# Attention with a bias: a dozen products moved from VectorE to GpSimd, a reordered start and a reordered end

## The chip, the cores and the metric

The kernel runs on one core of a Trainium2 chip. The metric is the device time of one execution in microseconds, lower is better. Times below are medians of several runs. Runs of one kernel agree within 1%, most far closer, with an exception that matters below: the kernel before took about 256.3 us instead of 253.6 in 7 of 31 runs.

The engines are called as the profile calls them: PE is TensorE (PEld its weight loads), ACT is ScalarE, DVE is VectorE, POOL is GpSimd, SP is SyncE.

## The reference

Batch 4, 8 heads, sequence 1024, head size 64. All heads share one bias.

```python
scores = scale * np.matmul(q, k.transpose(0, 1, 3, 2))
scores = scores + bias
scores_max = np.max(scores, axis=-1, keepdims=True)
attn = np.exp(scores - scores_max) / (np.sum(np.exp(scores - scores_max), axis=-1, keepdims=True) + 1e-8)
return np.matmul(attn, v)
```

The kernel uses exp(s + b) = exp(s) * exp(b). It computes exp(bias) once, stores it in `eb`, and multiplies every block of exponentials by it. The row sum comes from a column of ones beside V.

## The kernel before

The unit of work is a bank: 128 keys by 512 queries of one head. There are 512 banks, in groups of 16 (one head pair and one half of the queries; the two heads alternate). ACT exponentiates three banks at a time (a slot), DVE multiplies two at a time (a pair), and PE multiplies each bank with V.

```python
banks = [(pr, h, qh, kc) for pr in range(NP) for qh in range(2) for kc in range(NCH) for h in range(2)]
slots = [[0], [1, 2]] + [list(range(i, min(i + 3, NB))) for i in range(3, NB, 3)]
...
def s_fill(g):                        # PE: scores of one slot into PSUM, two slots deep
    for j, b in enumerate(slots[g]):
        nc.tensor.matmul(ps[:, j, :], kT[:, kc, :], qT[:, h, qh * HQ:(qh + 1) * HQ], start=True, stop=True)

def s_exp(g):                         # ACT: exponential, PSUM to SBUF
    nc.scalar.activation(e_at(slots[g][0], n), open_ps.pop(("S", g))[:, :n, :], ACTF.Exp, scale=scale)

def mul_pair(b, n=2):                 # DVE: two SBUF inputs, 128 x 1024 bf16
    e = e_at(b, n)
    nc.vector.tensor_tensor(e, e, eb[:, qh, kc:kc + 1, :].to_broadcast([P, n, HQ]), op=ALU.mult)
...
for i in range(8):                    # prologue: warm-up matmuls
    nc.tensor.matmul(wm[:, i % 3, :], zeros[:, :P], zeros[:], start=True, stop=True)
...                                   # k_first, q_first: casts, transposes and copies of the first blocks
k_first(0, nc.scalar.copy, nc.scalar.copy)
q_first(0, nc.vector.tensor_copy)
s_fill(0)
s_exp(0)
q_first(1, nc.vector.tensor_copy)
s_fill(1)
s_exp(1)
k_first(2, nc.vector.tensor_copy, nc.vector.tensor_copy)
```

The order of everything after the prologue is found while the program is written: a small model with a clock for ACT, PE and DVE picks the next instruction of each engine. Each engine then runs its list in order, so an instruction that comes late holds up all that stand behind it on its engine.

The softmax here doesn't subtract the row's maximum and nothing guards it: scores larger than these inputs give would overflow.

## Time and profile before

| | before |
|---|---|
| time, median of 3 (range) | 253.62 us (253.60 to 253.69) |
| span of the profiled run (which took 254.24 us) | 252.5 us |
| first exponential begins | 6.20 us |
| three-bank exponentials without a gap from | 8.96 us, three banks done |
| last exponential ends | 244.74 us |
| from there to the end | 7.8 us |

These are two lines of the page's list of groups. The columns after the bar are busy microseconds and the mean ns of one instruction, then the idle time in front of the group and what ended it.

```profile
L130 ACT ACTIVATE E<-ps 128x1536 bf16<-128x1536 f32 (+2 forms) x172 | 230.1, 1668 | 2.1 <-PE ps L125 2.1
L148 DVE TENSOR_TENSOR E<-E,eb 128x1024 bf16<-128x1024 bf16 x256 | 163.5, 683 | 1.0 <-ACT eb L143 1.0
```

ACT's exponentials of scores waited only 2.1 us in the whole run. A product lasts 0.68 us, but overlaps the next: 163.5 / 256 = 0.64 us of busy time each, and a new one can begin every 0.60 us.

The windows view of the kernel before gives busy microseconds and, in brackets, instructions of each engine in a stretch of 30 us.

```profile
core 0: us, PE busy (x) PEld busy (x) DVE busy (x) ACT busy (x) POOL busy (x), PEclk, DMA share, GB/s
60.00:90.00 30.00, 28.38 (x386) 17.19 (x392) 28.69 (x59) 30.00 (x23) 6.33 (x8) 1.00 0.65 91
210.00:240.00 30.00, 28.30 (x388) 17.97 (x391) 29.08 (x60) 30.00 (x24) 0.00 (x0) 1.00 0.13 49
```

ACT is the bound, at 30.00 of 30. DVE with 28.7 to 29.1 has almost no slack.

The start, from the timelines of PE and ACT before (start, duration, engine, line, operation, output and input, count, idle time in front):

```profile
1.23 3.40 PE L209 MATMUL wm<-zeros 128*128 128x512 bf16 x8 [1.23 <-DVE zeros L184]
4.56 0.30 PE L217 MATMUL px<-ident,kr 128*64 128x128 bf16 x4
7.86 1.06 PE L125 MATMUL ps<-qT,kT 128*128 128x512 bf16 x3
```

```profile
6.20 0.60 ACT L130 ACTIVATE E<-ps 128x512 bf16<-128x512 f32 x1 [0.92 <-PE ps L125]
7.65 1.02 ACT L130 ACTIVATE E<-ps 128x1024 bf16<-128x1024 f32 x1 [0.85 <-PE ps L125]
8.96 6.82 ACT L130 ACTIVATE E<-ps 128x1536 bf16<-128x1536 f32 x5 [0.28 <-PE ps L125]
```

And the end, from its timeline:

```profile
243.42 1.32 ACT L130 ACTIVATE E<-ps 128x1024 bf16<-128x1024 f32 x1
244.47 3.09 DVE L148 TENSOR_TENSOR E<-E,eb 128x1024 bf16<-128x1024 bf16 x5
247.62 0.42 PE L160 MATMUL po<-vall,E 128*128 128x65 bf16 x8 [0.19 <-DVE E L148]
```

When ACT is done at 244.74 us, DVE still has almost all of five products before it. They, not the last exponential, set the end.

### The profile page before, as it was taken

How to read it: one execution, taken by the hardware profiler on the slowest of the kernel's cores; microseconds unless marked ns; L12 is line 12 of the kernel's file. 1: busy time of each engine (PE TensorE's matmuls, PEld its weight loads, DVE VectorE, ACT ScalarE, POOL GpSimd, SP SyncE). 2: the span in 40 equal slices, each digit the busy share in tenths (PEclk: the TensorE clock that was granted, in tenths of full speed). 3: DMA queues.
4: the chain of work that ended last, by engine and by line, in shares of the span. 5: the costliest groups of instructions: out<-in, count | busy, mean ns of one | idle time of the engine just before them, and what ended most of it. 6: DMA issues, size and time to landing. Idle time of an engine off the chain costs nothing.

```text
span 252.5 us, 7217 instructions
## 1 busy us (share of the span) xinstructions
PE 229.4 (91%) x3090; PEld 141.6 (56%) x3144; DVE 226.3 (90%) x461; ACT 239.1 (95%) x180; POOL 52.6 (21%) x72
## 2 busy tenths in 40 slices
PE   7768999999999999999999999999999999999982
PEld 2346646665565566565555566565555655555651
DVE  5319799999999999999999999999999999999993
ACT  3899999999999999999999999999999999999970
POOL 6652445022310513013042204034000000000000
PEclk9999999999999999999999999999999999999998
DMA  7999999749291589439196904939020201111112
GB/s 147 171 214 187 191 138 161 90 106 104 66 148 40 105 67 150 64 71 139 42 141 47 187 8 95 118 85 166 5 84 3 86 0 44 44 43 44 49 36 83
DMA packets 47744, 23.79 MB, mean 94 GB/s; under 512 B 34401, under 2 KB 43361, under 8 KB 47457
## 3 DMA queue, kind: packets, MB, share of 16 engines
q0 software_dynamic: 42272, 14.42, 52.7%
q1 hardware_dynamic: 5296, 8.78, 9.6%
q8 instruction: 24, 0.39, 0.7%
q10 hardware_dynamic: 144, 0.13, 0.2%
q14 instruction: 8, 0.06, 0.1%
HBM read 29.36 MB, written 8.39 MB: 150 GB/s over the span
## 4 chain that ended last, share of the span: by engine, by line
PE 44%; ACT 35%; DVE 10%; DMA 4%; issue 3%; POOL 1%; ACTq 1%
ACT E L130 33%; PE ps L125 30%; PE po L160 8%; DVE E L148 6%; PE px L88 6%; DMA qr<-in_q_dram 4%; ACT eb L143 2%; DVE oall L171 1%; DVE qT L97 1%; POOL vall L80 1%; DVE mask L199 1%; DVE rs L170 1%; ACTq L130 1%; PE pb L138 0%; POOL kr L74 0%
## 5 line engine op out<-in xcount | busy, mean ns | idle before, releaser
L130 ACT ACTIVATE E<-ps 128x1536 bf16<-128x1536 f32 (+2 forms) x172 | 230.1, 1668 | 2.1 <-PE ps L125 2.1
L148 DVE TENSOR_TENSOR E<-E,eb 128x1024 bf16<-128x1024 bf16 x256 | 163.5, 683 | 1.0 <-ACT eb L143 1.0
L125 PE MATMUL ps<-qT,kT 128*128 128x512 bf16 x458 | 134.5, 378 | 12.9 <-ACT E L130 4.7
L160 PEld LDWEIGHTS <-E 128*128 128x128 bf16 x2048 | 84.7, 98 | 40.3 <-DVE E L148 2.6
L160 PE MATMUL po<-vall,E 128*128 128x65 bf16 x2048 | 96.4, 194 | 2.4 <-DVE E L148 1.0
L125 PEld LDWEIGHTS <-kT 128*128 128x128 bf16 x512 | 45.3, 96 | 43.1 <-issue 10.2
L74 POOL DMA_DIRECT2D kr<-in_k_dram x15 | 10.5, 699 | 96.4 <-PE px L88 91.5
L171 DVE TENSOR_TENSOR oall<-po,rs 128x256 f32<-128x256 f32 x64 | 27.2, 425 | 2.4 <-DVE rs L170 0.3
L80 POOL DMA_DIRECT2D vall<-in_v_dram x32 | 28.1, 882 | 6.0 <-DMA btraw<-in_bias_dram 4.0
L97 DVE TENSOR_TENSOR qT<-px,mask 128x1024 bf16<-128x1024 bf16 x31 | 21.3, 688 | 2.3 <-PE px L88 1.6
L101 DVE COPY kT<-px 128x512 bf16<-128x512 bf16 x31 | 13.1, 424 | 10.5 <-PE px L88 9.7
L75 POOL DMA_DIRECT2D qr<-in_q_dram x15 | 10.7, 716 | 17.3 <-PE px L88 16.7
L170 DVE RECIPROCAL rs<-po 128x4 f32<-128x4 f32 x64 | 11.4, 179 | 3.1 <-PE po L160 2.7
L88 PE MATMUL px<-ident,qr 128*64 128x128 bf16 x248 | 12.8, 224 | 1.0 <-DMA qr<-in_q_dram 0.9
L88 PE MATMUL px<-ident,kr 128*64 128x128 bf16 x248 | 12.8, 225 | 0.2
L88 PEld LDWEIGHTS <-kr 128*64 128x64 bf16 x248 | 7.9, 109 | 8.5 <-issue 5.2
L88 PEld LDWEIGHTS <-qr 128*64 128x64 bf16 x248 | 8.0, 109 | 8.2 <-issue 6.4
L143 ACT ACTIVATE eb<-pb 128x2048 bf16<-128x2048 bf16 x4 | 7.5, 1881 | 0.6 <-PE pb L138 0.6
L138 PE MATMUL pb<-ident,btraw 128*128 128x128 bf16 x64 | 4.6, 225 | 0.9 <-ACT E L130 0.7
L138 PEld LDWEIGHTS <-btraw 128*128 128x128 bf16 x64 | 4.5, 147 | 1.5 <-issue 1.2
L209 PE MATMUL wm<-zeros 128*128 128x512 bf16 x8 | 3.4, 607 | 1.2 <-DVE zeros L184 1.2
L209 PEld LDWEIGHTS <-zeros 128*128 128x128 bf16 x8 | 1.0, 142 | 2.9 <-issue 1.6
(27 smaller groups left out, 13.3 us busy)
## 6 DMA issues: line engine op xcount, KB each, us to landing
out_dram<-oall SPq DMA_DIRECT2D x32, 256.0 KB, 2.5
vall<-in_v_dram POOLq DMA_DIRECT2D x32, 128.0 KB, 6.0
kr<-in_k_dram POOLq DMA_DIRECT2D x15, 256.0 KB, 4.2
qr<-in_q_dram POOLq DMA_DIRECT2D x15, 256.0 KB, 5.2
btraw<-in_bias_dram POOLq DMA_DIRECT2D x2, 1024.0 KB, 12.6
k0f<-in_k_dram SPq DMA_DIRECT2D x2, 128.0 KB, 3.3
q0f<-in_q_dram ACTq DMA_DIRECT2D x1, 128.0 KB, 2.5
q0f<-in_q_dram SPq DMA_DIRECT2D x1, 128.0 KB, 2.6
```

The costliest lines, as they stand in the source:

```text
L75: nc.gpsimd.dma_start(out=qr.rearrange("p t c d -> p t (c d)"), in_=qf[pr])
L80: nc.gpsimd.dma_start(out=vall[:, 2 * pr + t, :, :D], in_=vf[pr, :, t])
L88: nc.tensor.transpose(px[t * D:(t + 1) * D, c, :], src[:, t, half * QC + c, :], ident[:])
L97: nc.vector.tensor_tensor(dst[:, :, half * HQ:(half + 1) * HQ], px.rearrange("p c q -> p (c q)").unsqueeze(1).to_broadcast([P, 2, HQ]), ma ...
L101: nc.vector.tensor_copy(dst[:, half * QC:(half + 1) * QC, :], px[:])
L125: nc.tensor.matmul(ps[:, j, :], kT[:, kc, :], qT[:, h, qh * HQ:(qh + 1) * HQ], start=True, stop=True)
L130: nc.scalar.activation(e_at(slots[g][0], n), open_ps.pop(("S", g))[:, :n, :], ACTF.Exp, scale=scale)
L143: nc.scalar.activation(eb[:, qh, k0:k0 + 4, :], open_ps.pop(("B", qh, k0))[:, :4, :], ACTF.Exp)
L148: nc.vector.tensor_tensor(e, e, eb[:, qh, kc:kc + 1, :].to_broadcast([P, n, HQ]), op=ALU.mult)
L160: nc.tensor.matmul(acc[:, i, :], e[:, 0, i * P:(i + 1) * P], vall[:, 2 * pr + h, kc, :], start=(kc == 0 and i == 0), stop=(kc == NCH - 1), ...
L170: nc.vector.reciprocal(rs[:], acc[:, :, D:D1])
L171: nc.vector.tensor_tensor(oall[:, qh * QC:(qh + 1) * QC, :], acc[:, :, :D], rs[:].to_broadcast([P, QC, D]), op=ALU.mult)
```

## The change

The intent: begin ACT's stream earlier, take enough products from DVE that it finishes with ACT, and shorten what follows the last exponential. The core of the diff (cuts marked):

```diff
+    banks[NB - 16:] = [(NP - 1, h, 1, kc) for h in range(2) for kc in range(NCH)]
+    late_bias = {NB - 2: 0, NB - 1: 1}
+    slots = [[0], [1, 2], [3]] + [list(range(i, min(i + 3, NB))) for i in range(4, NB, 3)]
...
+            if b in late_bias:
+                nc.tensor.matmul(ps[:, j, :], ident[:], braw[:, late_bias[b], :], start=False, stop=True)
...
-    def mul_pair(b, n=2):
+    def mul_pair(b, n=2, eng=nc.vector):
...
+            if b == NB - 1:                      # last evacuation: half DVE and SP, half ACT
+                m = QC // 2
+                nc.vector.tensor_tensor(oall[:, c0:c0 + m, :], acc[:, :m, :D], ...)
+                nc.sync.dma_start(...)
+                for i in range(m, QC):
+                    nc.scalar.mul(oall[:, c0 + i, :], acc[:, i, :D], rs[:, i, :])
+                nc.scalar.dma_start(...)
...
-        for i in range(8):
+        for i in range(6):
             nc.tensor.matmul(wm[:, i % 3, :], zeros[:, :P], zeros[:], start=True, stop=True)
...
+        k_first(0, nc.scalar.copy, nc.scalar.copy, "xb")
+        c_a = q_first(0, "xa")
+        c_b = q_first(1, "xb")
+        c_a()
+        c_b()
         s_fill(0)
         s_exp(0)
+        k_first(2, nc.vector.tensor_copy, nc.vector.tensor_copy, "xa")
+        for g in range(1, 3):
+            s_fill(g)
+            s_exp(g)
...
+        def pool_pick():                         # DVE three pairs behind: the last of them to GpSimd
+            b, n, last = mul_next, 0, None
+            while b + 1 in exp_at and banks[b][2:] in eb_at:
+                if b not in pool_has and max(exp_at[b + 1], eb_at[banks[b][2:]]) <= max(t_pool, t_dve):
+                    n, last = n + 1, b
+                b += 2
+            if n < 3:
+                return None
+            ...
+                mul_pair(b, eng=nc.gpsimd)
+                mul_at[b] = mul_at[b + 1] = t + POOLMUL      # POOLMUL = 2100 ns
```

The model gives GpSimd a clock of its own.

More of the change, by code (lines that the diff above doesn't have):

```diff
@@ L60 @@
     eb = consts.tile([P, 2, NCH, HQ], BF)
+    braw = consts.tile([P, 2, HQ], BF)
     mask = consts.tile([P, 2, HQ], BF)
@@ L106 @@
     NB = len(banks)
-    slots = [[0], [1, 2]] + [list(range(i, min(i + 3, NB))) for i in range(3, NB, 3)]
+    banks[NB - 16:] = [(NP - 1, h, 1, kc) for h in range(2) for kc in range(NCH)]
+    late_bias = {NB - 2: 0, NB - 1: 1}
+    slots = [[0], [1, 2], [3]] + [list(range(i, min(i + 3, NB))) for i in range(4, NB, 3)]
     NS = len(slots)
@@ L112, in e_at @@
     def e_at(b, n):
+        b = b + 2
         if b // ET not in etiles:
@@ L125, in s_fill @@
             nc.tensor.matmul(ps[:, j, :], kT[:, kc, :], qT[:, h, qh * HQ:(qh + 1) * HQ],
-                             start=True, stop=True)
+                             start=True, stop=b not in late_bias)
+            if b in late_bias:
+                nc.tensor.matmul(ps[:, j, :], ident[:], braw[:, late_bias[b], :], start=False, stop=True)
     def s_exp(g):
@@ L143, in b_exp, with late_bias_pe, copy @@
         nc.scalar.activation(eb[:, qh, k0:k0 + 4, :], open_ps.pop(("B", qh, k0))[:, :4, :], ACTF.Exp)
-    def mul_pair(b, n=2):
+    def mul_pair(b, n=2, eng=nc.vector):
         pr, h, qh, kc = banks[b]
         e = e_at(b, n)
-        nc.vector.tensor_tensor(e, e, eb[:, qh, kc:kc + 1, :].to_broadcast([P, n, HQ]), op=ALU.mult)
+        if banks[b + 1][1] == h:
+            eng.tensor_tensor(e, e, eb[:, qh, kc:kc + n, :], op=ALU.mult)
+        else:
+            eng.tensor_tensor(e, e, eb[:, qh, kc:kc + 1, :].to_broadcast([P, n, HQ]), op=ALU.mult)
+    def late_bias_pe(tag):
+        px = ps_x.tile([P, 2, HQ], BF, tag=tag, name="px")
+        for j in range(2):
+            for i in range(QC):
+                nc.tensor.transpose(px[:, j, i * P:(i + 1) * P],
+                                    btraw[:, QC + i, :].rearrange("p (kp kc) -> p kc kp", kc=NCH)[:, NCH - 2 + j, :],
+                                    ident[:])
+        def copy():
+            nc.vector.tensor_scalar(braw[:], px[:], 1.0 / scale, None, op0=ALU.mult)
+        return copy
     oalls = {}
@@ L170, in evac @@
             nc.vector.reciprocal(rs[:], acc[:, :, D:D1])
-            nc.vector.tensor_tensor(oall[:, qh * QC:(qh + 1) * QC, :], acc[:, :, :D],
+            c0 = qh * QC
+            if b == NB - 1:
+                m = QC // 2
+                nc.vector.tensor_tensor(oall[:, c0:c0 + m, :], acc[:, :m, :D],
+                                        rs[:, :m, :].to_broadcast([P, m, D]), op=ALU.mult)
+                nc.sync.dma_start(out=of[2 * pr + h][:, c0:c0 + m, :], in_=oall[:, c0:c0 + m, :])
+                for i in range(m, QC):
+                    nc.scalar.mul(oall[:, c0 + i, :], acc[:, i, :D], rs[:, i, :])
+                nc.scalar.dma_start(out=of[2 * pr + h][:, c0 + m:c0 + QC, :], in_=oall[:, c0 + m:c0 + QC, :])
+                return
+            nc.vector.tensor_tensor(oall[:, c0:c0 + QC, :], acc[:, :, :D],
                                     rs[:].to_broadcast([P, QC, D]), op=ALU.mult)
-            if qh == 1:
+            if pr == NP - 1:
+                nc.sync.dma_start(out=of[2 * pr + h][:, c0:c0 + QC, :], in_=oall[:, c0:c0 + QC, :])
+            elif qh == 1:
                 nc.sync.dma_start(out=of[2 * pr + h], in_=oall[:])
@@ L207, with k_first @@
         wm = ps_s.tile([P, 3, HQ], F32, tag="s", name="wm")
-        for i in range(8):
+        for i in range(6):
             nc.tensor.matmul(wm[:, i % 3, :], zeros[:, :P], zeros[:], start=True, stop=True)
-        def k_first(c0, cast, copy):
+        def k_first(c0, eng_cast, eng_copy, tag):
             cs = slice(c0, c0 + 2)
-            cast(kr0[:, :, cs, :], k0f[:, :, cs, :])
-            px = ps_x.tile([P, 2, P], BF, tag="xb", name="px")
+            eng_cast(kr0[:, :, cs, :], k0f[:, :, cs, :])
+            px = ps_x.tile([P, 2, P], BF, tag=tag, name="px")
             for c in range(2):
@@ L217, in k_first, with q_first @@
                     nc.tensor.transpose(px[t * D:(t + 1) * D, c, :], kr0[:, t, c0 + c, :], ident[:])
-            copy(kT0[:, cs, :], px[:])
-        def q_first(t, copy):
+            eng_copy(kT0[:, cs, :], px[:])
+        def q_first(t, tag):
             nc.vector.tensor_copy(qr0[:, t, :QC, :], q0f[t][:])
-            px = ps_x.tile([P, QC, P], BF, tag="xa", name="px")
+            px = ps_x.tile([P, QC, P], BF, tag=tag, name="px")
             for c in range(QC):
                 nc.tensor.transpose(px[t * D:(t + 1) * D, c, :], qr0[:, t, c, :], ident[:])
-            copy(qT0[t * D:(t + 1) * D, t, :HQ], px[t * D:(t + 1) * D, :, :].rearrange("p c q -> p (c q)"))
-        k_first(0, nc.scalar.copy, nc.scalar.copy)
-        q_first(0, nc.vector.tensor_copy)
+            return lambda: nc.vector.tensor_copy(qT0[t * D:(t + 1) * D, t, :HQ],
+                                                 px[t * D:(t + 1) * D, :, :].rearrange("p c q -> p (c q)"))
+        k_first(0, nc.scalar.copy, nc.scalar.copy, "xb")
[3 more added lines that the diff above has]
+        c_b()
         s_fill(0)
         s_exp(0)
-        q_first(1, nc.vector.tensor_copy)
-        s_fill(1)
-        s_exp(1)
-        k_first(2, nc.vector.tensor_copy, nc.vector.tensor_copy)
+        k_first(2, nc.vector.tensor_copy, nc.vector.tensor_copy, "xa")
+        for g in range(1, 3):
+            s_fill(g)
+            s_exp(g)
         EXP, EXP0, QK, AV, TP = 427, 45, 216, 170, 350
         MUL, COPYQ, COPYK, EVAC, SEM = 600, 650, 420, 620, 80
-        order = [("S", g) for g in range(2, NS)]
+        POOLMUL = 2100
+        order = [("S", g) for g in range(3, NS)]
         for at, x in ((5, (0, 0)), (7, (0, 4)), (11, (1, 0)), (13, (1, 4))):
@@ L243 @@
         NO = len(order)
-        T0 = 9000.0
-        t_act, t_pe, t_dve = T0 + 900, T0, T0
+        T0 = 7500.0
+        t_act, t_pe, t_dve = T0 + 700, T0, T0 + 500
         filled = []
         act_end = []
-        x_free = {"xa": T0, "xb": T0}
+        x_free = {"xa": T0 + 500, "xb": T0}
         x_unit = {}
         bias_at = [13500, 22000]
-        raw_at = {0: 7000, 1: 17500, 2: 27500}
+        raw_at = {0: (6000, 7500), 1: (17200, 18300), 2: (26000, 28500)}
         pieces = [(0, 1, 1), (0, 0, 1)]
@@ L254 @@
             pieces += [(pr, 1, 0), (pr, 0, 0), (pr, 1, 1), (pr, 0, 1)]
+        pieces.append((NP, 0, 0))
+        raw_at[NP] = (T0, T0)
         piece_end = {(0, 1, 0): T0, (0, 0, 0): T0}
         eb_at = {}
-        exp_at = {0: T0 + 400, 1: T0 + 900, 2: T0 + 900}
+        exp_at = {0: T0, 1: T0 + 700, 2: T0 + 700, 3: T0 + 700}
         mul_at = {}
         mul_next = 0
+        pool_has = set()
+        t_pool = 30000.0
         av_order = []
@@ L293, in pe_fill @@
                     pr, h, qh, kc = banks[b]
-                    for key in ((pr, 1, kc // QC), (pr, 0, qh)):
+                    for key in ((pr, 1, kc // QC), (pr, 0, qh)) + (((NP, 0, 0),) if b in late_bias else ()):
                         if key not in piece_end:
@@ L297, in pe_fill @@
                         ready = max(ready, piece_end[key] + SEM)
-                cost = QK * len(slots[item[1]])
+                cost = QK * (len(slots[item[1]]) + sum(b in late_bias for b in slots[item[1]]))
             else:
@@ L314, in pe_piece @@
             pr, which, half = pieces[0]
-            if pr not in raw_at or pr not in raws:
+            if pr not in raw_at or (pr < NP and pr not in raws):
                 return None
@@ L331, in pe_piece @@
             free, tag = tags[0]
-            ready = max(free + SEM, raw_at[pr])
+            ready = max(free + SEM, raw_at[pr][1 - which])
             def emit(t):
                 pieces.pop(0)
-                copy = transpose_pe(pr, which, half, tag)
+                copy = transpose_pe(pr, which, half, tag) if pr < NP else late_bias_pe(tag)
                 cost = COPYK if which else COPYQ
@@ L340, in run @@
                 def run(t2):
+                    nonlocal t_pool
                     copy()
@@ L343, in run @@
                     piece_end[(pr, which, half)] = t2 + cost
-                    if which == 0 and half == 1:
+                    if pr < NP and which == 0 and half == 1:
                         if pr + 3 < NP:
                             load_qk(pr + 3)
-                            raw_at[pr + 3] = t2 + 7000
+                            t_pool = max(t_pool, t2) + 2200
+                            raw_at[pr + 3] = (t2 + 7000, t2 + 7000)
                         if pr + 2 < NP:
                             load_v(pr + 2)
+                            t_pool = max(t_pool, t2) + 2200
                 dve_q.append((t + TP + SEM, 0, cost, run))
@@ L401, in pe_pick, with emit @@
             return best
+        def pool_pick():
[6 more added lines that the diff above has]
+                return None
+            b = last
+            def emit(t):
+                mul_pair(b, eng=nc.gpsimd)
+                pool_has.add(b)
+                mul_at[b] = mul_at[b + 1] = t + POOLMUL
+            return max(t_pool, t_dve - MUL, exp_at[b + 1] + SEM), POOLMUL, emit
         def dve_pick():
             nonlocal mul_next
+            while mul_next in pool_has:
+                mul_next += 2
             c = list(dve_q)
-            if mul_next < NB:
+            if mul_next < NB and mul_next not in late_bias:
                 pr, h, qh, kc = banks[mul_next]
@@ L435 @@
                 c.append((p[0], 2))
+            g = pool_pick()
+            if g:
+                c.append((g[0], 3))
             t, who = min(c)
@@ L445 @@
                         exp_at[b] = t_act
+                        if b in late_bias:
+                            mul_at[b] = t_act
                 else:
@@ L454 @@
                 d[3](t)
+            elif who == 3:
+                t_pool = t + g[1]
+                g[2](t)
             else:
```

## The prediction

> **What bounds it now.** ScalarE. The windows view shows ACT busy 30.00 of 30 us in every stretch from 30 to 240 us; a three-bank exponential starts every 1.34 us (timeline: 16 in 21.46 us). From 8.96 to 244.74 us ACT idles only 0.56 us. VectorE is nearly as full: 28.7 to 29.1 us of each 30; a pair's product (128x1024) starts every 0.60 us. So time can be won only before ACT's continuous stream (8.96 us, three banks done), after its end (244.74 to 252.5 us, 7.8 us), or by letting VectorE finish with ACT: at 244.47 it still owes five products (3.09 us), then two evacuations.
>
> **What the change does.**
> 1. Prologue. Two warm-up matmuls fewer (0.43 us each): the first K transposes start at 4.56 us though their cast ended at 3.97, so they come about 0.5 us earlier. Both Q casts and transposes run before either copy, so VectorE no longer waits 0.50 and 0.57 us. But the first Q cast (about 4.5 us, behind 0.9 us of VectorE idle put down to "issue") stays, so the first exponential stays near 6.2 us, and the K cast now stands in front of the second fill. Estimate: 0.5 us gained (0 to 1.3).
> 2. About 12 products move to GpSimd: VectorE loses 12 x 0.60 = 7.2 us. That alone shortens nothing (ACT bounds), but clears the backlog at the end. No trace here shows a product on GpSimd; the Trainium skill, "GPSIMD Engine Reference", section 3.1, gives about 2.6 cycles an element for two inputs: an estimate of 2.2 us for 1024 columns.
> 3. Last group head by head, the last two banks' bias on TensorE (two matmuls of 0.22 us, eight transposes, one VectorE copy, in TensorE's slack of about 5%). Behind the last exponential no product remains.
> 4. One slot more: 0.06 us on ACT (1.34 less 3 x 0.427).
> 5. Tail after the last exponential: four products with V 0.42, reciprocal 0.2, the slower half of the evacuation, on ACT, about 0.5, then store and finish as before, 252.5 - 249.14 = 3.4 us. Sum 4.5 to 4.7 against 7.8: 3.1 us gained, all on the critical path.
>
> Total: 253.62 - 3.1 - 0.5 + 0.06 = about 250.0; I shade to 249.7, since the prologue may give more.
>
> **Predicted: 249.7 us, 80% range 247.6 to 252.8.** Faster by over 2%: 0.18; within 2%: 0.73; slower by over 2%: 0.09.
>
> **Checks in the profile after.** ACT's stream gapless, period 1.34 us, ending 0 to 1.3 us earlier; first exponential near 6.2 us; about 12 GpSimd products of 2 to 2.5 us; VectorE busy about 219 us; no product after the last exponential; last exponential to end about 4.6 us.
>
> **What would make it wrong.** The Trainium skill, "SBUF — State Buffer", section "SBUF: two separate sides", says that VectorE and GpSimd share a port pair as an exclusive lock: a VectorE operation with two SBUF inputs and a GpSimd operation that reads SBUF block each other entirely. The product is such an operation. If that holds fully, each GpSimd product blocks VectorE's for about 2 us and saves 0.6: up to 12 x 1.5 = 18 us more on an engine without slack, TensorE (in order) waits for late products, ACT for TensorE: above 258. VectorE products far above 0.68 us beside GpSimd's would show it. I think it unlikely to decide, because products go to GpSimd only when VectorE is three pairs behind, and evacuations from PSUM can fill part of the wait. Fewer warm-up matmuls may also leave TensorE slow for longer (granted clock in the first slices).

## The result, and the profile after

| | before | after |
|---|---|---|
| time, median of 6 (range) | 253.66 us (253.60 to 256.30) | 270.33 us (269.24 to 271.84) |
| span of the profiled run | 252.5 us | 268.9 us |
| three-bank exponentials without a gap from | 8.96 us, 3 banks done | 13.26 us, 7 banks done |
| last exponential ends | 244.74 us | 263.69 us |
| from there to the end | 7.8 us | 5.2 us |

The ratio is 1.065 (95% interval 1.059 to 1.070), so 6.5% slower. A ratio here is the mean time of one kernel's fast runs over that of the other's fast runs of the same rounds, so it is not quite the ratio of the medians. The result is correct.

The groups of the page after that answer to those of before:

```profile
L137 ACT ACTIVATE E<-ps 128x1536 bf16<-128x1536 f32 (+1 forms) x173 | 232.4, 1493 | 19.8 <-PE ps L130 15.5
L158 DVE TENSOR_TENSOR E<-E,eb 128x1024 bf16<-128x1024 bf16 x236 | 172.0, 767 | 9.5 <-ACT eb L150 8.0
L158 POOL TENSOR_TENSOR E<-E,eb 128x1024 bf16<-128x1024 bf16 x12 | 26.7, 2232 | 69.0 <-ACT E L137 62.6
L156 DVE TENSOR_TENSOR E<-E,eb 128x1024 bf16<-128x1024 bf16 x7 | 4.7, 690 | 0.3
```

DVE does 243 products (236 + 7) instead of 256: 12 went to GpSimd, and TensorE adds the bias of one pair. Yet DVE is busy with them for 172.0 + 4.7 = 176.7 us instead of 163.5. At 0.64 us each, 243 would have taken 155.2, so 21.5 us were added. Part of this is only that the products overlap each other less than before; by the means of the group, 236 x (767 - 683) ns, they were stopped for 19.8 us, 1.65 us for each of the 12 GpSimd products, against 13 x 0.64 = 8.3 us saved. The waiting of ACT's exponentials grew from 2.1 to 19.8 us, 15.5 of it put down to PE.

One GpSimd product, from the timeline after:

```profile
90.77 0.69 DVE L98 TENSOR_TENSOR qT<-px,mask 128x1024 bf16<-128x1024 bf16 x1
90.83 2.12 POOL L158 TENSOR_TENSOR E<-E,eb 128x1024 bf16<-128x1024 bf16 x1 [3.83 <-ACT E L137]
91.38 2.12 DVE L158 TENSOR_TENSOR E<-E,eb 128x1024 bf16<-128x1024 bf16 x1
```

The POOL product runs from 90.83 to 92.95. The DVE product that begins at 91.38 ends only at 93.50, that is 0.55 us after POOL's end. After each of the 12 GpSimd products of this trace, the stopped DVE product ends 0.55 us after it. The operation at 90.77, with one operand in PSUM (`px`) and one in SBUF, ran beside POOL in its usual 0.69 us. Note that the blocked time is recorded as busy time of DVE, so DVE's share of the span (89%) shows nothing of the stop; the mean of the group, 767 ns instead of 683, does.

The worst place holds three GpSimd products in a row. First the timeline after, then the windows view of the same stretch (columns as before).

```profile
51.44 7.17 POOL L158 TENSOR_TENSOR E<-E,eb 128x1024 bf16<-128x1024 bf16 x3 [1.35 <-ACT E L137]
52.21 6.95 DVE L158 TENSOR_TENSOR E<-E,eb 128x1024 bf16<-128x1024 bf16 x3
59.77 0.64 PE L89 MATMUL px<-ident,kr 128*64 128x128 bf16 x8 [4.28 <-DVE oall L205]
62.33 1.45 ACT L137 ACTIVATE E<-ps 128x1536 bf16<-128x1536 f32 x1 [5.36 <-PE ps L130]
```

```profile
52.00:56.00 4.00, 2.80 (x36) 1.36 (x34) 4.00 (x3) 3.87 (x4) 4.00 (x2) 1.00 0.98 67
56.00:60.00 4.00, 0.23 (x6) 0.24 (x8) 3.97 (x5) 0.97 (x1) 2.61 (x2) 0.77 0.00 0
60.00:64.00 4.00, 4.00 (x38) 2.37 (x35) 2.96 (x7) 1.45 (x1) 0.76 (x1) 0.50 0.58 130
```

Three DVE products took 6.95 us. GpSimd was stopped too: its second and third product here lasted 2.56 us each instead of 2.12, and each began while a DVE product was under way and ended 1.98 us after it. PE, which works in order, waited 4.28 us for an evacuation behind them, and ACT waited 5.36 us for PE. After this idle time PE ran on half the clock (0.50 in the last window), which stretched the recovery. The Trainium skill, "TensorE: Matmul & The Clock Gate", Part 1, says that the clock is halved after an idle window of about 3.4 us; this trace does not fit that figure: its clock record falls to 0.50 at 58.17 us, only 2.7 us into the gap of 4.28 us. In b_pool_only (below) the clock fell after PE gaps of 2.36 and 1.81 us.

The start after, on PE and on ACT:

```profile
1.23 2.74 PE L245 MATMUL wm<-zeros 128*128 128x512 bf16 x6 [1.23 <-DVE zeros L220]
4.06 0.42 PE L253 MATMUL px<-ident,kr 128*64 128x128 bf16 x4
7.25 1.46 PE L130 MATMUL ps<-qT,kT 128*128 128x512 bf16 x3
```

```profile
6.63 0.60 ACT L137 ACTIVATE E<-ps 128x512 bf16<-128x512 f32 x1 [1.73 <-PE ps L130]
8.32 1.51 ACT L137 ACTIVATE E<-ps 128x1024 bf16<-128x1024 f32 x2 [1.10 <-PE ps L130]
10.88 1.45 ACT L137 ACTIVATE E<-ps 128x1536 bf16<-128x1536 f32 x1 [1.04 <-PE ps L130]
13.26 5.48 ACT L137 ACTIVATE E<-ps 128x1536 bf16<-128x1536 f32 x4 [0.94 <-PE ps L130]
```

The first transposes do come 0.5 us earlier (4.06), but they take 0.42 instead of 0.30 us, and three score matmuls take 1.46 instead of 1.06 or less. PE stays slow until 13.8 us, where the trace's first record of the full clock begins, and the exponentials wait for it one by one.

The end after:

```profile
261.67 2.02 ACT L137 ACTIVATE E<-ps 128x1536 bf16<-128x1536 f32 x2
262.49 1.43 DVE L156 TENSOR_TENSOR E<-E,eb 128x1024 bf16<-128x1024 bf16 x2
264.90 0.29 DVE L198 TENSOR_TENSOR oall<-po,rs 128x128 f32<-128x128 f32 x1
265.27 0.52 ACT L202 ACTIVATE oall<-po,rs 128x64 f32<-128x64 f32 x2 [1.58 <-PE po L183]
```

Here the change does what it was meant to do: the last product ends at 263.92, 0.2 us after the last exponential, and 7.8 us have become 5.2.

**Theory.** A GpSimd operation that reads SBUF and a DVE operation with two SBUF inputs exclude each other for the whole instruction. DVE has no slack, so every GpSimd product costs more than it saves. The slower start is PE's clock.

**Rivals.** (a) Nothing is blocked; PE waits because GpSimd's results come late, or because products in one tile wait for each other. (b) The new order of the work costs the time. (c) In the start, the new order of casts and fills costs the time, not the clock.

### The profile page after: what moved, and what is told of

It reads as the page before. It is cut to its first block, busy times and chain, and to the rows that moved or that the text cites. A ratio compares the mean times of both kernels' runs of the same rounds, so it can differ in the third digit from the quotient of the medians.

```text
span 268.9 us, 7308 instructions
## 1 busy us (share of the span) xinstructions
PE 232.9 (87%) x3152; PEld 142.1 (53%) x3152; DVE 238.9 (89%) x449; ACT 241.8 (90%) x183; POOL 79.8 (30%) x84
## 4 chain that ended last, share of the span: by engine, by line
DVE 36%; PE 33%; ACT 21%; issue 6%; DMA 1%; POOL 1%; ACTq 0%; POOLq 0%
DVE E L158 24%; PE ps L130 21%; ACT E L137 19%; PE po L183 7%; PE px L89 5%; DVE qT L98 4%; DVE oall L205 3%; ACT eb L150 3%; DMA kr<-in_k_dram 1%; DVE rs L193 1%; DVE kT L102 1%; DVE mask L235 1%; POOL vall L81 0%; DVE qT L261 0%; POOL qr L76 0%
## 5 line engine op out<-in xcount | busy, mean ns | idle before, releaser
L137 ACT ACTIVATE E<-ps 128x1536 bf16<-128x1536 f32 (+1 forms) x173 | 232.4, 1493 | 19.8 <-PE ps L130 15.5
L158 DVE TENSOR_TENSOR E<-E,eb 128x1024 bf16<-128x1024 bf16 x236 | 172.0, 767 | 9.5 <-ACT eb L150 8.0
L130 PE MATMUL ps<-qT,kT 128*128 128x512 bf16 x512 | 142.0, 387 | 6.2 <-ACT E L137 3.7
L183 PE MATMUL po<-vall,E 128*128 128x65 bf16 x2048 | 98.1, 195 | 13.3 <-DVE E L158 11.0
L130 PEld LDWEIGHTS <-kT 128*128 128x128 bf16 x512 | 43.7, 98 | 36.6 <-issue 9.2
L158 POOL TENSOR_TENSOR E<-E,eb 128x1024 bf16<-128x1024 bf16 x12 | 26.7, 2232 | 69.0 <-ACT E L137 62.6
L89 PE MATMUL px<-ident,qr 128*64 128x128 bf16 x248 | 13.2, 230 | 2.3 <-DVE oall L205 1.1
L156 DVE TENSOR_TENSOR E<-E,eb 128x1024 bf16<-128x1024 bf16 x7 | 4.7, 690 | 0.3
```

The lines of the kernel that those rows point to most:

```text
L89: nc.tensor.transpose(px[t * D:(t + 1) * D, c, :], src[:, t, half * QC + c, :], ident[:])
L158: eng.tensor_tensor(e, e, eb[:, qh, kc:kc + 1, :].to_broadcast([P, n, HQ]), op=ALU.mult)
L183: nc.tensor.matmul(acc[:, i, :], e[:, 0, i * P:(i + 1) * P], vall[:, 2 * pr + h, kc, :], start=(kc == 0 and i == 0), stop=(kc == NCH - 1), ...
```

## The experiments

Eleven kernels ran. In each group I name the edit, the expectation, and the measurement. All times stand beside the kernel before on the same chip (median 253.6 to 253.8 us).

### GpSimd's products taken away from the kernel after

```diff
-            if n < 3:
-                return None
+            return None
```

> The kernel after with its 12 GpSimd products given back to VectorE, everything else kept. Port lock theory (a product on GpSimd stops VectorE's products while it runs): the about 14 us of ACT idle time after 32 us vanish, what stays is the slower prologue (ACT's continuous stream about 2.5 us behind the kernel before) and the shorter tail (about -2.6 us): 253 to 255 us. Rival, the new order of the work (head by head, bias on TensorE, changed model constants) costs the time: stays above 262 us.

Measured: 256.06 us (254.72 to 257.24), 14.3 us under the kernel after. From 32.41 us on, ACT's timeline is one line of 160 exponentials without a gap:

```profile
32.41 214.20 ACT L137 ACTIVATE E<-ps 128x1536 bf16<-128x1536 f32 x160
```

Rival (b) falls: 2.4 of the 16.7 us remain with the new order, and the warm-ups below explain part of them. The value is 1 us above the range that I expected, because the tail did not get shorter after all (see a_nopool_wm8).

### GpSimd's products put alone into the kernel before

The edit adds `pool_pick` and GpSimd's clock to the model of the kernel before, and nothing else.

> The kernel before with the GpSimd products alone (the same rule for choosing them gives 8 here), prologue, order and tail unchanged. Port lock theory: VectorE products beside them take about 2 us instead of 0.68, ACT idles about 1.2 us per GpSimd product: +8 to +12 us, 261 to 266 us. Rival, GpSimd products are harmless by themselves: 253 to 254 us, or less.

Measured: 267.44 us (267.36 to 267.47), +13.8 us, just above the range on record. That text counts 8 products; that was a miscount of mine, and the trace has 12. So it is 1.15 us for each, the size on record (about 1.2). The products alone carry 13.8 of the 16.7 us.

### Products on GpSimd that nobody waits for

On the kernel before; DVE keeps all of its 256 products. A tiny copy of two columns ties each operation to a moment in the stream.

```diff
         nc.vector.tensor_tensor(e, e, eb[...].to_broadcast([P, n, HQ]), op=ALU.mult)
+        if b % 34 == 0 and 60 <= b < 460:            # 12 times
+            nc.gpsimd.tensor_copy(tick[:], e[:, 0, :2])
+            nc.gpsimd.tensor_tensor(scc[:, :2 * HQ], sca[:, :2 * HQ], scb[:, :2 * HQ], op=ALU.mult)
```

> The kernel before with 12 products (128x1024 bf16) on GpSimd on scratch tiles that nobody reads, each started by a VectorE product; VectorE keeps all 256 products. Port lock theory: each one stops VectorE about 2 us although nothing waits for its result; VectorE has no slack, so +12 to +22 us, 266 to 276 us, VectorE products up to 2.1 us long beside them. Rival, the time is lost because TensorE waits for GpSimd's late results (or for a dependency between the products by tile), not by a conflict: 253.6 us as before.

Measured: 272.35 us (271.13 to 273.87), +18.7 us, 1.56 us for each. The groups of this kernel, and one place of its timeline:

```profile
L152 DVE TENSOR_TENSOR E<-E,eb 128x1024 bf16<-128x1024 bf16 x256 | 185.8, 769 | 1.0 <-ACT eb L147 1.0
L155 POOL TENSOR_TENSOR scc<-sca,scb 128x1024 bf16<-128x1024 bf16 x12 | 26.4, 2197 | 0.0
```

```profile
155.65 2.12 POOL L155 TENSOR_TENSOR scc<-sca,scb 128x1024 bf16<-128x1024 bf16 x1
155.82 0.42 DVE L178 TENSOR_TENSOR oall<-po,rs 128x256 f32<-128x256 f32 x1
156.16 2.76 DVE L152 TENSOR_TENSOR E<-E,eb 128x1024 bf16<-128x1024 bf16 x2
```

No engine uses `scc`, and these products share no tile with DVE's. DVE's products still took 185.8 - 163.5 = 22.3 us more, 1.86 us for each. Rival (a) falls: late results and dependencies play no part in this kernel, and it is about as slow as the kernel after. The evacuation at 155.82, whose large operand lies in PSUM, again ran beside POOL in its usual 0.42 us.

### What of the GpSimd operation does the blocking

The same insertion with a memset of 128x2048 (writes, reads nothing), then with a copy of 128x2048 (one SBUF input).

```diff
-            nc.gpsimd.tensor_tensor(scc[:, :2 * HQ], sca[:, :2 * HQ], scb[:, :2 * HQ], op=ALU.mult)
+            nc.gpsimd.memset(scc[:], 1.0)             # b_dummy_memset
+            nc.gpsimd.tensor_copy(scc[:], sca[:])     # b_dummy_copy
```

> As b_dummy_mul, but the 12 GpSimd operations are memsets of 128x2048 bf16 on scratch (1.82 us each in b_dummy_mul's trace), which write SBUF and read none of it. If only a GpSimd operation that reads SBUF stops a VectorE product (as the skill's page has it): 253.6 to 254.5 us, VectorE products stay at 0.68 us. If any use of SBUF by GpSimd does: +10 us or more.

> As b_dummy_mul, but the 12 GpSimd operations are copies of 128x2048 bf16 from scratch to scratch: one SBUF input. If one SBUF read is enough to stop a VectorE product: longest products about 0.6 us longer than the copy's duration, and 12 times about (copy duration - 0.5 us) more: 265 us or more if the copy takes 1.8 us or more. If it takes two reads on GpSimd: 253.6 us.

Measured: memset 253.60 us (253.57 to 253.83), as before; copy 267.89 us (267.13 to 269.74), +14.1 us. The groups with the memset, then with the copy:

```profile
L152 DVE TENSOR_TENSOR E<-E,eb 128x1024 bf16<-128x1024 bf16 x256 | 163.5, 683 | 1.0 <-ACT eb L147 1.0
L155 POOL MEMSET scc<- 128x2048 bf16 x12 | 21.6, 1804 | 0.0
```

```profile
L152 DVE TENSOR_TENSOR E<-E,eb 128x1024 bf16<-128x1024 bf16 x256 | 182.8, 758 | 1.0 <-ACT eb L147 1.0
L155 POOL COPY scc<-sca 128x2048 bf16<-128x2048 bf16 x12 | 23.7, 1972 | 0.0
```

Memset and copy last about as long (1.80 and 1.89 us at the median), and only the copy stops DVE: 182.8 - 163.5 = 19.3 us, 1.6 us for each. The tiny copy that starts each operation stands in both kernels, so it does no harm either. Writing from GpSimd is harmless to these products; reading SBUF, even with one input, is not. This is what the Trainium skill, "SBUF — State Buffer", section "SBUF: two separate sides", says of a VectorE operation with two SBUF inputs. One half of the rule is not tested here: the DVE operations that ran on unharmed all had an operand in PSUM. None with a single SBUF input and no PSUM operand stood beside a GpSimd read, so the runs do not show that it takes two SBUF inputs on DVE's side.

### The warm-up matmuls

First, the kernel after without GpSimd products, with eight warm-ups again:

```diff
-        for i in range(6):
+        for i in range(8):
```

> As a_nopool, and eight warm-up matmuls again instead of six; the new order of the prologue stays. If the two missing warm-ups kept TensorE at half speed until about 11 us (matmul spacing 0.43 us instead of 0.22): spacing 0.22 us from about 5 us on, ACT's stream continuous near 9.5 us, 2 to 2.5 us faster than a_nopool, about 251 us. If instead the new order (K cast in front of the second fill) costs the time: same as a_nopool within 0.5 us.

Then the kernel before with six for eight, nothing else:

> The kernel before with six warm-up matmuls for eight, nothing else. If six are too few to bring TensorE to full speed (theory): first matmuls spaced 0.43 us until about 10 to 11 us, ACT's continuous stream 1.5 to 2.5 us later, 255 to 256 us. Rival, in a_nopool the new order of the prologue made it slow: 253.2 to 253.7 us.

Measured: a_nopool_wm8 254.67 us (254.56 to 255.26), 1.4 us under a_nopool. b_wm6 255.96 us (254.75 to 256.18), 2.2 us over the kernel before by the medians. Rival (c) falls for the larger part: in the profile of a_nopool_wm8, with eight warm-ups and the new order, the first transposes take 0.30 us again and the first exponential begins at 6.20.

```profile
4.63 0.30 PE L253 MATMUL px<-ident,kr 128*64 128x128 bf16 x4
```

These medians mix two kinds of runs. The spans of a_nopool's four runs are 254.9, 254.9, 252.8 and 252.8 us, those of a_nopool_wm8 252.8 in all four: a slow start costs 2.1 us here, and six warm-ups do not always bring it. All six runs of b_wm6 have 253.0 to 254.4 us. In the batches of the experiments the kernel before, with eight warm-ups, has 251.8 to 252.3 in 19 runs and 254.5 in 6. So six warm-ups make a slow start likelier, and eight do not rule it out.

In b_wm6's profile PE was not cold from the beginning. Its windows view:

```profile
3.00:6.00 3.00, 1.89 (x12) 0.54 (x10) 1.59 (x5) 0.78 (x2) 1.57 (x3) 1.00 1.22 194
6.00:9.00 3.00, 2.48 (x14) 0.86 (x13) 1.29 (x3) 1.62 (x2) 3.00 (x5) 0.74 0.92 174
```

It was fast at 4 us (four transposes in 0.30 us) and lost its clock at 7.43 us for 3.41 us, with no PE gap over 0.56 us in the 3.4 us before. In the kernel after it was slow from the start, and yet the windows view shows a granted clock of 1.00 there. The trace has no clock record before 13.80 us, and the column counts time without a record as 1.00. So it misses a cold start, and the spacing of the matmuls has to be read. Why six warm-ups go wrong in two ways, I have not shown. The 256.3 us runs of the kernel before were not traced, so it is not shown that they are such starts. But one such start with eight warm-ups was: in b_dummy_copy's profile, the slowest of its four runs, PE is at half rate until 13.58 us. In the other nine profiles with eight warm-ups the full clock comes between 4.31 and 6.84 us.

My expectation of 251 us for a_nopool_wm8 was missed. Its end shows why:

```profile
246.55 1.28 DVE L156 TENSOR_TENSOR E<-E,eb 128x1024 bf16<-128x1024 bf16 x2
...
249.18 0.52 ACT L202 ACTIVATE oall<-po,rs 128x64 f32<-128x64 f32 x2 [4.66 <-PE po L183]
```

ACT's exponentials end at 244.52, but DVE's last product ends at 247.83. Without relief DVE is as late as before, and the new tail gains nothing.

### Relief for nothing

The kernel after with eight warm-ups; the 12 GpSimd products are not done by anyone. Its output is wrong, which doesn't matter for the time.

```diff
             def emit(t):
-                mul_pair(b, eng=nc.gpsimd)
                 pool_has.add(b)
```

> Wrong result on purpose: the kernel after with eight warm-ups, and its 12 GpSimd products left out altogether (VectorE does not do them either), the order of everything else as in after. This is the world that the prediction assumed: relief of VectorE for nothing. If the lock is the whole of the slowdown and the tail works as predicted: no ACT idle time in mid-stream, no product owed after the last exponential, last exponential to end 4.6 to 5.2 us, 251 to 252 us, about 3 us under a_nopool_wm8. If the order of the schedule itself costs time: 254 us or more.

Measured: 251.84 us (251.51 to 252.37). The exponentials end at 244.71 and the span at 249.9, so 5.2 us. Every instruction list is that of the kernel after, but for two warm-ups more and 12 products on GpSimd fewer. The 270.33 us shrink by 18.5. The warm-up is 1.4 of them by the medians of the pair above (2.1 for a run with a slow start), so 16 to 17 are the GpSimd products, about 1.4 us each.

### Relief from TensorE instead

In every second head pair (odd `pr`), the bias of two banks more is added in PSUM, from a scaled copy `braw0` that DVE makes near 15 us, when it has nothing to do.

```diff
+    pe_bias = {b: kc for b, (pr, h, qh, kc) in enumerate(banks) if qh == 0 and kc == 0 and pr % 2 == 1}
...
+            if b in pe_bias:
+                nc.tensor.matmul(ps[:, j, :], ident[:], braw0[:, pe_bias[b], :], start=False, stop=True)
```

> A candidate: after without GpSimd products, eight warm-ups, and VectorE relieved by TensorE instead: in every second head pair the bias of two banks more (one product of VectorE less, two matmuls of 0.22 us more) is added in PSUM, from a bias copy made while VectorE is idle near 15 us. 8 products fewer, 4.8 us of VectorE. If the products owed at the end are what keeps a_nopool_wm8 from the tail's gain: 251 to 252.2 us. If TensorE has no room for the 16 matmuls: 254 us or more, ACT waiting for PE.

Measured: 252.05 us (251.96 to 252.05), ratio 0.990. (The ratio goes by means, and two of the seven runs of the kernel before took 256.3 us; the medians give 0.993.) The end:

```profile
243.18 2.04 DVE L160 TENSOR_TENSOR E<-E,eb 128x1024 bf16<-128x1024 bf16 x3
...
246.19 0.29 DVE L202 TENSOR_TENSOR oall<-po,rs 128x128 f32<-128x128 f32 x1
246.57 0.52 ACT L206 ACTIVATE oall<-po,rs 128x64 f32<-128x64 f32 x2 [1.59 <-PE po L187]
```

DVE's last product ends at 245.22, 0.2 us after the last exponential at 244.98. Eight products fewer did what twelve on GpSimd were meant to do, and TensorE had room for 16 matmuls (ACT's waits stayed at 2.2 us in all).

### Two smaller parts of the change

The last evacuation undivided again (the branch `if b == NB - 1` removed):

> best8 without the split of the last evacuation: VectorE alone multiplies all 256 columns (0.43 us) and SyncE stores them. In best8's trace the ScalarE half begins only after the VectorE half (246.57 after 246.48) and its store is issued at 247.12; one product of 0.43 us from 246.19 would let the store be issued at about 246.65. If the split costs rather than gains: 0.2 to 0.4 us faster, about 251.7 us. If the smaller stores land sooner and pay for it: 252.1 us or more.

Measured: 251.79 us (251.68 to 251.87). The ranges of the two kernels do not meet, though they ran in different batches, so the 0.26 us is probable rather than sure: the split does not pay.

On top of that, the prologue in the order of before:

> best8_nosplit with the prologue in the order of the kernel before (Q half, first fill, other Q half, second fill, then the K part), eight warm-ups, first four banks still as slots of 1, 2, 1. In a_nopool_wm8 the new order began the second exponential at 7.77 us (7.65 in the kernel before) and the three-bank stream at 9.69 us with four banks done (8.96 with three done, so the fourth's worth of 0.45 leaves it 0.28 us behind). If the new order is the worse one: 0.1 to 0.4 us faster than best8_nosplit. If it is worth something: slower.

Measured: 251.66 us (251.56 to 252.05), against 251.79 in the same batch, with ranges that overlap. The new order of the prologue is worth nothing either way. This is the best version, and correct: ratio 0.990 to the kernel before (0.987 to 0.994), 0.992 by the medians.

## Why the prediction was wrong

1. *What bounds it* held. After the first 20 us, ACT's stream has no gap over 0.1 us in any kernel traced without GpSimd products or copies of whole tiles, and DVE without slack is what made the blocking visible in the time.
2. *The step that failed* is the last one: "I think it unlikely to decide, because products go to GpSimd only when VectorE is three pairs behind, and evacuations from PSUM can fill part of the wait." With it went item 2 of its sum: "VectorE loses 12 x 0.60 = 7.2 us" became 13.2 us more of busy time on products (163.5 to 176.7). The mechanism stood in the text, with "up to 18 us". The runs showed it nearly whole: 1.65 us of stopped products for each GpSimd product in the kernel after, 1.86 in b_dummy_mul, and +13.8, +18.7 and about +17 us in three kernels. Being three pairs behind does not protect DVE; it means that DVE has products to do, and those are what is stopped. The filling by evacuations is real, but small: a GpSimd product lasts 2.12 us and only 0.3 to 0.5 us of it was hidden (2.12 less 1.86 or 1.65).
3. *GpSimd's own duration* was right: estimated 2.2 us, measured 2.12 us. The Trainium skill, "GPSIMD Engine Reference", section 3.1, gave a good figure for the wrong question.
4. *Prologue*, "0.5 us gained (0 to 1.3)", was wrong in sign. I counted the warm-ups only as a delay of the first transposes, and named a slow PE as a mere risk. With two fewer, PE ran at half speed early on in most runs: by the medians 1.4 us lost in one pair of kernels and 2.2 us in the other. The order of the prologue gained nothing (251.79 against 251.66).
5. *Tail*, "3.1 us gained", had the right mechanism and was a little too large: with relief for nothing the stretch after the last exponential measured 5.2 us, not 4.6, so 2.6 us gained. One part of the gap is the split evacuation, whose ACT half began only after the DVE half (246.57 after 246.48 in best8). That relief of DVE is a condition for this gain, as the prediction said, is shown by a_nopool_wm8 (none of it gained) and best8 (all of it gained).
6. The prediction's own world exists as a_ghost_wm8: 251.84 us against my 250.0 before shading. Of the missing 1.8 us, 0.6 is the tail (point 5) and about 0.4 the start: with eight warm-ups the exponentials still ended at 244.71, where the forecast comes to 244.3 (244.74 - 0.5 + 0.06). About 0.6 lies in the prediction's sum, which took its stretches from a profiled run of 254.24 us and subtracted them from the median of 253.62.

## What to carry to other kernels

Before moving elementwise work from VectorE to GpSimd, ask what VectorE will be doing meanwhile: if it is operations with two SBUF inputs, expect a GpSimd operation that reads SBUF to stop them for most of its length, as a product and a copy did here (1.6 to 1.86 us of about 2), so the move pays only if VectorE has other work for that time. Look for relief on an engine that does not stop VectorE (here TensorE, adding the bias in PSUM), and test an engine's effect on its neighbour with an operation whose result nobody needs. When a page of the Trainium skill names a conflict that fits the change exactly, treat it as the expected case, not as a footnote.

## What the Trainium skill lacked or had wrong

- "SBUF — State Buffer", section "SBUF: two separate sides": the lock is stated rightly. It does not say how a profile shows the stop, which is recorded as busy time of the stopped instruction: here products of 0.68 us appear as up to 2.62 us in the kernel after and 3.19 us in b_dummy_mul, and VectorE's share of the span stays at 89%.
- "GPSIMD Engine Reference", section 4.1, calls a two-input operation on GpSimd about 2 times slower than on VectorE. For this bf16 product it is 2.12 us against one every 0.60 us, 3.5 times.
- "TensorE: Matmul & The Clock Gate", Part 1, gives about 3.4 us of idle time for the halved clock. Here less was enough: 2.7 us in the kernel after, gaps of 2.36 and 1.81 us in b_pool_only. From the first warm-up matmul (1.23 us) to the first record of the full clock it took 2.8 to 5.6 us in ten profiles and about 12 us in three (the kernel after, a_nopool, b_dummy_copy). The page warns that clock events in traces are unreliable. It does not name the case met here: no record at all while the matmuls are at half rate, as in the first 13.8 us of the kernel after (0.43 us between matmuls of 512 columns).
